# The second score product of a neighbourhood attention, on 64 rows and on all 128

## The chip, the core and the metric

The kernel runs on one core of a Trainium2 chip. The metric is the time of one execution on the device in microseconds (us). The engines named here: TensorE (PE, with its weight loads as PEld), VectorE (DVE), ScalarE (ACT), GpSimd (POOL) and SyncE (SP), whose queue issues all of this kernel's DMAs.

## What is computed

Two layers of a diffusion block work on 512 latent tokens (a grid of 8 rows and 64 columns) and, in the first layer, on 256 context tokens as well. Each layer has a mixer of three kinds side by side (Fourier mixing, retention with four heads, neighbourhood attention with six heads of 64), an output projection and a feed-forward part. The part that matters here:

```python
def neighborhood_attention(q, k, v, k_ctx, v_ctx, rpb):
    ...  # each block of 16 query columns sees a window of 32 key columns in all 8 rows
    s_lat = einsum('brjqhd,brjkhd->bhrjqk', qb, kg) * scale + bias[None]
    s_ctx = einsum('brjqhd,bchd->bhrjqc', qb, k_ctx) * scale
    p = softmax(concatenate([s_lat, s_ctx], axis=-1), axis=-1)
    out = einsum(p_lat, vg) + einsum(p_ctx, v_ctx)
```

In the first layer the context tokens have an attention of their own over the context keys.

## The kernel before

**Split operands.** Products have float32 accuracy from float32r operands: each operand is kept as a high part and a low part, and `mm3` (lines 398 to 400) adds three products, without that of the two low parts. The high part is made by ScalarE (a cast) and the low part by VectorE or GpSimd (a subtraction). For the weights this is `put`: the cast at line 183 (`wh`) and the subtraction at line 188 (`wl`), the latter on GpSimd for nearly all of them.

**The keys and queries of the neighbourhood attention.** A pair of heads shares the 128 rows of a tile, 64 rows each (`HALVES`). `na_evac_q` gives each head a query tile with the high parts in the head's own rows and the low parts in the other 64. `na_evac_k` gives each head a key tile whose high parts stand in both halves (the second by a DMA), and puts the low parts of both heads into one third tile, each in its own rows. So the first product of a score, all 128 rows of the query against the high keys, holds high times high and low times high, and the second needs high times low only: it takes the head's own 64 rows of the query and of the low keys. `mm2` in `score` issues the two (lines 1086 and 1087), and they add up in one PSUM place.

**Blocks.** A head has four blocks of 128 latent queries, and in the first layer a fifth item for the context queries. `score` issues four matmuls for a block: two pairs of 256 columns, or, for the last block of queries (`b == 3`), a pair of 384 and a pair of 128. Then `soft` adds the bias and takes the row's bound on VectorE (line 1074) and the exponent on ScalarE (line 1077), `scale` divides on VectorE (lines 1117 and 1118), `transp` turns the block by four transposes on TensorE (`nt`, line 1129), `parts` splits it (lines 403 and 404, `pt`), and `values` multiplies by the values (`nav`, line 1151). A block is scaled one block later and transposed three blocks later (`NL, SL = 3, 1`).

**The order of the work.** The program's order is written out: `beside` runs two generators side by side, the projections (products `proj`, `v`, `res`) and the attentions, and takes the next piece from the one or the other by the estimated TensorE time and the table `MIX`. So blocks of scores lie between pieces of projections. In each engine the order is fixed by this; the engines wait for each other by semaphores.

**Memory.** Tiles of 768 columns (tag `a`) share 40 places; a tile takes the place of one that is no longer used, and its first writer waits for the last reader of that one. The projected keys of the three pairs are made by `na_proj`, well ahead of their use in `neighbours`.

Of the kernel before, what the change touches and what calls it, by code (L numbers as in the profile page):

```python
# [7 lines left out]
F32 = mybir.dt.float32  # L8
F32R = mybir.dt.float32r
# [18 lines left out]
# feed-forward: pairs of chunks between two returns to the residual stream, by layer  # L28
# [5 lines left out]
# for each layer, where the parts of the attentions lie beside the projections: times after the ends of some;  # L34
# the four heads' retention, the readout, the three pairs' of heads neighbourhoods, the first values
# [5 lines left out]
# steps of the operands' preparation beside the first products  # L41
PREP = (0, 1, 1, 2), (1, 1, 1, 2)
# products of the two-by-two scheme in the order of their use
# half of the latent tokens, in the order of the columns, whose mirror images are the others
# [5 lines left out]
# columns of the vector blob  # L50
V_C, V_BADA, V_GMIX, V_GFFN, V_GFIN, V_RETG, V_DEC, V_SEL, V_RP, V_END = 0, 16, 112, 128, 144, 152, 158, 174, 176, 178
# columns of the constant blob
C_ID, C_BLK, C_END = 0, 128, 256
# columns of the decay strips: latent tiles, edge tile, context-context, context-latent
# [4 lines left out]
class Job:  # L59
    """a pair of chunks of outputs, from pairs of chunks of inputs and for two halves of the tokens, by seven  # L60
    products (Strassen's scheme in Winograd's form):
    P1 = A11 B11, P2 = A12 B21, P3 = S4 B22, P4 = A22 T4, P5 = S1 T1, P6 = S2 T2, P7 = S3 T3,
    S1 = A21 + A22, S2 = S1 - A11, S3 = A11 - A21, S4 = A12 - S2,
    T1 = B12 - B11, T2 = B22 - T1, T3 = B22 - B12, T4 = B21 - T2;
    C11 = P1 + P2, C12 = P1 + P6 + P5 + P3, C22 = P1 + P6 + P7 + P5, C21 = P1 + P6 + P7 + P4"""

# [6 lines left out]
def in_order(jobs, after, window):  # L73
    """the order of the jobs' steps on the tensor engine: the oldest job's first step whose operands are there;
    after[key, step]: pairs of another step and a delay"""
# [26 lines left out]
class WeightStream:  # L102
    """DMA of the weights in the order of their use, running ahead, and their split into two float32r parts."""

    SLOTS = 11
    # the units of a job that the weights of a product are made from
    USES = {1: (0,), 2: (0,), 3: (0,), 4: (1,), 5: (), 6: (0, 1), 7: (0, 1)}

    def __init__(self, kern, raws, parts):
        self.k = kern  # L110
        self.max_raws, self.max_parts = raws, parts
        self.units, self.tasks = [], []
        self.raw, self.parts, self.size, self.pending = {}, {}, {}, []
        self.when = {}
        self.n_dma = self.n_split = self.n_raw = self.n_parts = 0
        self.limit = 10**6
        # products whose weights' second parts are the vector engine's, of the first jobs and the others
        self.lead, self.dve = {}, {}
        # parts that may go to other places, and those that are there
        self.spare, self.away = 0, set()  # L120
# [5 lines left out]
    def add_step(self, job, p, aps):  # L126
        """the weights of one product of a job, from the two units of its outputs"""
# [8 lines left out]
    def issue(self):  # L136
        """start loads while there is room"""
# [28 lines left out]
    def part(self, n):  # L166
        """tiles for the two parts of n columns"""
# [23 lines left out]
    def split(self):  # L191
        """split the next unit, or put it aside for its callback"""
# [18 lines left out]
    def form(self, job, p):  # L211
        """the sums that the weights of product p are made from, and those after it"""
# [9 lines left out]
        if p == 6:  # L222
            # S2 takes the place of A11, S3 that of A21 and S4 that of A12
# [49 lines left out]
    def get(self, key):  # L273
        """the parts of a unit, to be followed by done() after its last use"""
        self.flush()
        self.pump()
        return self.parts.pop(key)
# [7 lines left out]
def beside(first, second, kern):  # L285
    """Run two generators side by side; each yields the tensor-engine time of what it has just emitted,
    which kern.pe adds up. The second also yields spans (from, to, cost): its next work lies between these
    times of the first."""
# [22 lines left out]
def pieces(st):  # L311
    """the latent and the context tokens of a stream: which, columns of all tokens, columns of the stream"""
# [7 lines left out]
class Norm:  # L320
    """a layer norm done step by step: the sums, the rows' factors, then a chunk at a time"""
# [28 lines left out]
class Kern:  # L350
# [10 lines left out]
    # ---- tiles  # L361
    def table(self, key, ap):
        """a table of 1024 columns, loaded ahead of its use"""
# [30 lines left out]
    # ---- products of split operands  # L394
    def mm3(self, out, a, b, start, stop):
        """out += a^T b for a = (hi, lo), b = (hi, lo) without the product of the two low parts"""
# [9 lines left out]
    # ---- set-up  # L406
# [18 lines left out]
    def decay_logs(self):  # L425
        """log_sigmoid of the decay logits: min(x, 0) - 2 atanh(z), z = e / (2 + e), e = exp(-|x|)"""
# [21 lines left out]
    # ---- adaLN modulation  # L448
    def ada_load(self, k):
        """weights of the first layer's first shift and scale for the features 8 p + k"""  # L450
# [9 lines left out]
    def ada_first(self, k):  # L460
        """the two's modulation of the features 8 p + k: four groups of columns of the tensor engine share
        the sums, the rows of one stream are then added and turned to partitions"""
# [39 lines left out]
    def ada_unit(self, layer, part, i):  # L502
        """a unit of the first layer's parts in use before its feed-forward, for the tensor engine;
        of the others, for the vector engine"""
# [7 lines left out]
    def silu_tables(self):  # L512
        """silu of the two conditions on all partitions"""
# [5 lines left out]
    def ada_dve(self, raw, layer, part, i):  # L519
        """modulation of the features 8 p + i: a row's products with the condition, summed"""  # L520
# [69 lines left out]
    # ---- layer norm with modulation  # L590
    def sumsq(self, x, m, acc, st):
        """add the squares of chunk m of the residual stream to the sums of acc, those of the last chunk beside them"""
# [8 lines left out]
    def rstd(self, acc, n, merge=True):  # L601
        """1 / RMS of the n tokens, on all partitions of a bank: roots and reciprocals are taken with
        the tokens on partitions"""
# [18 lines left out]
    def modulate(self, x, rs, st, layer, f, h):  # L622
        """h = x rstd g (1 + sc) + sh, split; a generator over the chunks"""
# [37 lines left out]
    # ---- projections  # L661
    def proj(self, key, h, streams, evac):
        """features on partitions: a chunk of 128 columns of the weight against the streams"""
# [18 lines left out]
    def proj_v(self, keys, h, out, norms=None, late=1, heads=False):  # L682
        """tokens on partitions: 384 columns of the weight for the six token tiles;
        with norms the latent tiles come first, beside the layer norms of the two streams"""
# [27 lines left out]
        if heads:  # L712
            # for each token tile the heads' parts side by side, the second of two heads with its low part first
# [17 lines left out]
    def evac_rope(self, dst, tab):  # L731
        """rotary embedding of the latent tokens; the pairs lie 16 partitions apart"""
# [18 lines left out]
    # ---- retention  # L751
    def strip_piece(self, layer, h, piece, delta, st):
        """decay factors of one piece of the strips, an engine's work at a time: delta holds its distances,
        st takes them"""
# [4 lines left out]
        if piece == "cx":  # L759
            # from the context's state in either direction  # L760
# [13 lines left out]
        # both directions have the diagonal  # L774
# [9 lines left out]
    def pieces(self, work):  # L784
        """strip pieces (layer, head, piece, delta, st), a step behind one another"""
# [16 lines left out]
    def strips_first(self):  # L802
        """the first layer's strips: the first head's stay, the others' go to DRAM"""
# [3 lines left out]
        # the distances  # L807
# [43 lines left out]
    def strips_ahead(self, layer, heads):  # L851
        """strips of a later layer, kept in DRAM"""
# [1393 lines left out]
```

## Time and profile before

| | |
|---|---|
| median of 3 runs | 1755.63 us |
| lowest and highest run | 1754.65 and 1760.47 us |
| span of the profiled execution | 1759.0 us |
| PE busy | 1655.9 us, 94% |
| DVE busy | 1219.6 us, 69% |
| POOL busy | 867.1 us, 49% |
| ACT busy | 744.6 us, 42% |
| mean granted TensorE clock | 0.978 |

The profile is of one execution, so durations from it belong to its span of 1759.0 us and not to the median of the runs. The busy time of an engine is the time in which at least one of its instructions is recorded as running; matmuls overlap in the records, so for PE the distance between the starts of two matmuls says more than their durations. The granted clock is the share of TensorE's full speed that the chip allowed.

### The profile page before, as it was taken

What the parts mean: (1) busy time and instruction counts of PE and PEld (TensorE: products, weight loads), DVE (VectorE), ACT (ScalarE), POOL (GpSimd) and SP (SyncE); (2) the same over time, 40 slices, a digit from 0 to 9 for tenths busy, and PEclk for the clock granted to TensorE, in tenths of its full rate; (3) what the DMA queues carried; (4) which work ended last, traced back from release to release, by engine and by line L of the source; (5) the groups of instructions that cost most, each with busy time, mean ns of one, the idle gap of its engine ahead of it and who ended that gap; (6) DMA issues with size and microseconds to landing.
All of it is one profiled execution on the core that took longest, in us unless ns stands there. A gap on an engine that the chain in (4) does not pass through costs nothing. (4 is left out here: it accounts for less than half of the span.)

```text
span 1759.0 us, 26982 instructions
## 1 busy us (share of the span) xinstructions
PE 1655.9 (94%) x10054; PEld 1481.4 (84%) x10054; DVE 1219.6 (69%) x2040; ACT 744.6 (42%) x1437; POOL 867.1 (49%) x621
## 2 busy tenths in 40 slices
PE   6989999999979998999999999999998799999997
PEld 4867777778978987798999997778788799999997
DVE  6866555664687899586776867764656877767585
ACT  5544434454453223232332554444554444334333
POOL 3343231022467557465665833532035787677673
PEclk9999999999989999999999999999999899999998
DMA  9354243244122343434343444422132232332222
GB/s 344 131 193 133 71 148 94 91 135 167 37 72 85 110 142 108 132 120 132 124 153 114 135 164 138 141 71 87 61 120 73 66 103 87 95 109 84 64 94 72
DMA packets 76387, 202.33 MB, mean 115 GB/s; under 512 B 12704, under 2 KB 19488, under 8 KB 75872
## 3 DMA queue, kind: packets, MB, share of 16 engines
q1 hardware_dynamic: 76256, 200.60, 35.0%
q8 instruction: 80, 1.31, 0.3%
q14 instruction: 51, 0.42, 0.1%
HBM read 184.25 MB, written 11.80 MB: 111 GB/s over the span
## 5 line engine op out<-in xcount | busy, mean ns | idle before, releaser
L188 POOL TENSOR_TENSOR wp<-wr,wp 128x512 fp32r<-128x512 f32 (+1 forms) x336 | 477.5, 1433 | 275.4 <-ACT wp L183 271.8
L399 PE MATMUL f<-hp,wp 128*128 128x384 f32 (+1 forms) x1232 | 387.7, 315 | 13.9 <-POOL wp L188 7.6
L398 PE MATMUL f<-hp,wp 128*128 128x384 f32 (+1 forms) x1232 | 386.9, 314 | 14.5 <-DVE U L1598 5.3
L400 PE MATMUL f<-hp,wp 128*128 128x384 f32 (+1 forms) x1232 | 386.0, 313 | 3.9 <-POOL hp L1523 3.5
L183 ACT CAST wp<-wr 128x512 fp32r<-128x512 f32 (+1 forms) x360 | 213.0, 607 | 355.1 <-PE f L400 117.0
L188 POOL TENSOR_TENSOR wl<-wr,wh 128x1024 fp32r<-128x1024 f32 (+2 forms) x75 | 163.7, 2187 | 379.4 <-ACT wh L183 251.1
L399 PEld LDWEIGHTS f<-hp,wp 128*128 128x128 f32 x1232 | 238.3, 193 | 19.6 <-POOL wp L188 12.9
L398 PEld LDWEIGHTS f<-hp,wp 128*128 128x128 f32 x1232 | 238.6, 194 | 17.8 <-issue 9.7
L400 PEld LDWEIGHTS f<-hp,wp 128*128 128x128 f32 x1232 | 238.4, 194 | 5.2 <-POOL hp L1523 4.3
L398 PE MATMUL f<-g,wp 128*128 128x256 f32 (+1 forms) x576 | 183.6, 319 | 12.8 <-ACT g L1460 12.6
L400 PE MATMUL f<-g,wp 128*128 128x256 f32 (+1 forms) x576 | 183.3, 318 | 4.8 <-POOL g L1461 4.2
L399 PE MATMUL f<-g,wp 128*128 128x256 f32 (+1 forms) x576 | 182.4, 317 | 0.0
L398 PE MATMUL proj<-h,wh 128*128 128x512 f32 (+1 forms) x456 | 167.7, 368 | 0.9 <-DVE v L404 0.9
L399 PE MATMUL proj<-h,wl 128*128 128x512 f32 (+1 forms) x456 | 159.4, 350 | 0.7 <-POOL wl L188 0.7
L400 PE MATMUL proj<-h,wh 128*128 128x512 f32 (+1 forms) x456 | 159.1, 349 | 0.0
L1657 DVE SCALAR_TENSOR_TENSOR x<-f,mod,x 128x256 f32<-128x256 f32 (+1 forms) x160 | 83.8, 546 | 82.8 <-PE f L400 82.7
L398 PEld LDWEIGHTS f<-g,wp 128*128 128x128 f32 x576 | 113.2, 197 | 21.8 <-ACT g L1460 15.2
L400 PEld LDWEIGHTS f<-g,wp 128*128 128x128 f32 x576 | 113.0, 196 | 13.6 <-POOL g L1461 4.8
L399 PEld LDWEIGHTS f<-g,wp 128*128 128x128 f32 x576 | 113.4, 197 | 6.0
L522 DVE CUSTOM_DVE_ANT_0 adj<-wr,tab 128x1024 bf16<-128x1024 f32 x64 | 105.9, 1672 | 10.6 <-DMA wr<-in_w_adat_dram 10.6
L398 PEld LDWEIGHTS proj<-h,wh 128*128 128x128 f32 x456 | 86.6, 190 | 28.6 <-issue 8.3
L399 PEld LDWEIGHTS proj<-h,wl 128*128 128x128 f32 x456 | 86.9, 190 | 11.8 <-POOL wl L188 1.1
(251 smaller groups left out, 3510.1 us busy)
## 6 DMA issues: line engine op xcount, KB each, us to landing
wr<-in_w_dram SPq DMA_DIRECT2D x88, 512.0 KB
wr<-in_w_adat_dram SPq DMA_DIRECT2D x48, 512.0 KB
wr<-in_w_dram SPq DMA_DIRECT2D x80, 256.0 KB
wr<-in_w_ada_dram SPq DMA_DIRECT2D x32, 512.0 KB
ada<-in_w_ada_dram SPq DMA_DIRECT2D x16, 512.0 KB
wr<-in_w_out_dram SPq DMA_DIRECT2D x16, 512.0 KB
tab<-in_rpb_dram SPq DMA_DIRECT2D x12, 512.0 KB
strip<-strips SPq DMA_DIRECT2D x3, 1152.0 KB
```

Of the source, the lines that this page charges most:

```text
L183: nc.scalar.copy(hi, src)
L188: (nc.vector if vector else nc.gpsimd).tensor_sub(lo, src, hi.bitcast(F32))
L398: mm(out, a[0], b[0], start=start, stop=False)
L399: mm(out, a[1], b[0], start=False, stop=False)
L400: mm(out, a[0], b[1], start=False, stop=stop)
L522: self.nc.vector.tensor_tensor_reduce(out=self.tmp(mybir.dt.bfloat16, D, "adj"), in0=raw, in1=self.tabs[("silu", s)], scale=1.0, scalar=0. ...
L1657: k.nc.vector.scalar_tensor_tensor(xs, ps[:, :n], k.mod[:, self.layer, 5, s, m : m + 1], xs, op0=OP.mult, op1=OP.add)
```

## The change

The low parts of the keys get one tile for each head instead of one for the pair. In each, the head's own 64 rows hold the low parts as before, and the other 64 rows are set to zero by GpSimd. The second product of a score then takes all 128 rows of the query tile and of the low keys; the query's low parts meet the zeros. A pair of heads holds four key tiles in place of three. (Comments and docstrings also leave the file; the lines from the middle on have numbers that are one or two higher.)

```diff
     def na_evac_k(self, dst):
...
             for i, (own, other) in enumerate((HALVES, HALVES[::-1])):
                 hi = dst[i][own, c]
+                nc.gpsimd.memset(dst[2 + i][other, c].bitcast(F32), 0.0)
                 nc.scalar.copy(hi, ps[own, :n])
                 nc.sync.dma_start(dst[i][other, c].bitcast(F32), hi.bitcast(F32))
-                nc.vector.tensor_sub(dst[2][own, c], ps[own, :n], hi.bitcast(F32))
+                nc.vector.tensor_sub(dst[2 + i][own, c], ps[own, :n], hi.bitcast(F32))
...
         def score(h, b):
-            r = HALVES[h % 2]
             (q, q3, k), tab = head["qk"], head["tab"]
-            q, q3, kh, kl = q[h % 2], q3[h % 2], k[h % 2], k[2]
+            q, q3, kh, kl = q[h % 2], q3[h % 2], k[h % 2], k[2 + h % 2]
 
             def mm2(out, qb, c0, n):
                 c = slice(c0, c0 + n)
                 nc.tensor.matmul(out, qb, kh[:, c], start=True, stop=False)
-                nc.tensor.matmul(out, qb[r], kl[r, c], start=False, stop=True)
+                nc.tensor.matmul(out, qb, kl[:, c], start=False, stop=True)
...
         def na_proj(c):
...
-            kk = [k.act(F32R, name="nk") for _ in range(3)]
+            kk = [k.act(F32R, name="nk") for _ in range(4)]
```

On TensorE, VectorE, ScalarE and SyncE the instructions stand in the same order as before, with the same tiles' names and shapes of results. GpSimd's queue has 650 rows in place of 626. This is its place in the first layer where the first pair of heads gets its keys (`wl` are low parts of weights, `wr` and `wh` the weights and their high parts; `nq` the last block's queries, `nk` keys, `yr` the retention's readout), before:

```order
L1029 CAST nq_353_1870<-nq_1868 128x128
L1029 CAST nq_354_1871<-nq_1869 128x128
L188 TENSOR_TENSOR wl_1959<-wr_1720,wh_1958 128x768
L1010 TENSOR_TENSOR yr_1904<-yr_1904,osq_1909 128x768
L188 TENSOR_TENSOR wl_2051<-wr_1878,wh_2050 128x768
L1010 TENSOR_TENSOR yr_1905<-yr_1905,osq_1910 128x768
L188 TENSOR_TENSOR wl_2127<-wr_1977,wh_2126 128x768
```

The same place in the changed kernel:

```order
L1029 CAST nq_353_1870<-nq_1868 128x128
L1029 CAST nq_354_1871<-nq_1869 128x128
L188 TENSOR_TENSOR wl_1959<-wr_1720,wh_1958 128x768
L1046 MEMSET nk_1970 64x512
L1046 MEMSET nk_1971 64x512
L1010 TENSOR_TENSOR yr_1904<-yr_1904,osq_1909 128x768
L188 TENSOR_TENSOR wl_2054<-wr_1878,wh_2053 128x768
L1046 MEMSET nk_1970 64x256
L1046 MEMSET nk_1971 64x256
L1010 TENSOR_TENSOR yr_1905<-yr_1905,osq_1910 128x768
L188 TENSOR_TENSOR wl_2132<-wr_1978,wh_2131 128x768
```

Two memsets for the latent tokens (512 columns) and two for the context tokens (256) now stand ahead of a product of the readout and of a weight's low part. GpSimd's queue where the second and the third pair get their keys, before:

```order
L188 TENSOR_TENSOR wl_2516<-wr_2336,wh_2515 128x1024
L188 TENSOR_TENSOR wl_2652<-wr_2519,wh_2651 128x1024
L1029 CAST nq_472_2665<-nq_2663 128x128
L1029 CAST nq_473_2666<-nq_2664 128x128
L188 TENSOR_TENSOR wl_2764<-wr_2538,wh_2763 128x1024
L188 TENSOR_TENSOR wl_2924<-wr_2673,wh_2923 128x528
L188 TENSOR_TENSOR wl_3118<-wr_2783,wh_3117 128x528
```

And in the changed kernel, from the first of the second pair's memsets to the last but one of the third pair's:

```order
L1046 MEMSET nk_2532 64x512
L1046 MEMSET nk_2533 64x512
L188 TENSOR_TENSOR wl_2660<-wr_2524,wh_2659 128x1024
L1046 MEMSET nk_2532 64x256
L1046 MEMSET nk_2533 64x256
L1029 CAST nq_474_2675<-nq_2673 128x128
L1029 CAST nq_475_2676<-nq_2674 128x128
L188 TENSOR_TENSOR wl_2774<-wr_2544,wh_2773 128x1024
L1046 MEMSET nk_2785 64x512
L1046 MEMSET nk_2786 64x512
L188 TENSOR_TENSOR wl_2937<-wr_2683,wh_2936 128x528
L1046 MEMSET nk_2785 64x256
```

Here each low part of a weight has two memsets ahead of it. The second layer has the same pattern, so that 24 memsets are added in all.

## Rows read from the trace of the kernel before

**Rows 1.** The page's first block: busy time, share of the span, instructions.

```profile
span 1759.0 us, 26982 instructions
...
PE 1655.9 (94%) x10054; PEld 1481.4 (84%) x10054; DVE 1219.6 (69%) x2040; ACT 744.6 (42%) x1437; POOL 867.1 (49%) x621
```

**Rows 2.** Two stretches: length; PE, PEld, DVE, ACT, POOL busy; clock, DMA share, GB/s.

```profile
240.00:400.00 160.00, 157.73 (x857) 121.70 (x856) 92.43 (x236) 78.85 (x174) 28.97 (x18) 1.00 0.38 115
1180.00:1300.00 120.00, 117.60 (x603) 93.99 (x602) 67.75 (x160) 59.74 (x124) 26.03 (x17) 0.99 0.23 73
```

**Rows 3.** PE in time: start, duration, line, result and operands, rows*columns, moving operand.

```profile
243.68 0.33 PE L398 MATMUL v<-wh,h 128*128 128x384 f32 x1
...
244.72 0.28 PE L1086 MATMUL ns<-nk,nq 128*128 128x256 f32 x1
244.93 0.38 PE L1087 MATMUL ns<-nk,nq 64*128 64x256 f32 x1
245.24 0.38 PE L1086 MATMUL ns<-nk,nq 128*128 128x256 f32 x1
245.55 0.38 PE L1087 MATMUL ns<-nk,nq 64*128 64x256 f32 x1
245.86 0.44 PE L398 MATMUL v<-wh,h 128*128 128x384 f32 x1
246.14 0.34 PE L399 MATMUL v<-wh,h 128*128 128x384 f32 x1
...
247.01 0.28 PE L1086 MATMUL ns<-nk,nq 128*128 128x256 f32 x1
```

**Rows 4.** PE in time, output projection of the second layer; two more starts lie between.

```profile
1298.64 0.28 PE L400 MATMUL res<-ys,wh 128*128 128x256 f32 x1
...
1298.99 0.28 PE L400 MATMUL res<-ys,wh 128*128 128x256 f32 x1
```

**Rows 5.** PE in time, retention of the second layer; two more starts in each gap.

```profile
1137.11 0.39 PE L398 MATMUL rs<-rq,rk 96*128 96x512 f32 x1
...
1137.80 0.40 PE L398 MATMUL proj<-h,wh 128*128 128x512 f32 x1
...
1138.50 0.40 PE L398 MATMUL rav<-rah,v 128*96 128x512 f32 x1
```

**Rows 6.** PE in time, a block of the last queries; four more starts lie between.

```profile
251.60 0.34 PE L1086 MATMUL ns<-nk,nq 128*128 128x384 f32 x1
...
253.03 0.34 PE L399 MATMUL v<-wh,h 128*128 128x384 f32 x1
```

**Rows 7.** The line of the second product: least, median, greatest duration in ns; forms.

```profile
L1087 PE MATMUL ns<-nk,nq x108: 322/381/442, 244.9 to 1292.6; 64*128 64x256 f32 x84, 64*128 64x384 f32 x12, 64*128 64x128 f32 x12
```

**Rows 8.** Groups of POOL by form: count, busy us, mean ns, idle before and releasers.

```profile
L932 POOL TENSOR_TENSOR ral<-ra,rah 128x512 fp32r<-128x512 f32 x24 | 31.0, 1290 | 65.3 <-ACT rah L931 64.9 <-POOL wl L188 0.3
...
L1029 POOL CAST nq<-nq 128x128 fp32r<-128x128 f32 x12 | 3.5, 292 | 28.7 <-DVE nq L1024 28.7
```

**Rows 9.** In time: a weight's low part, and the first product that takes it.

```profile
287.40 2.40 POOL L188 TENSOR_TENSOR wl<-wr,wh 128x1024 fp32r<-128x1024 f32 x1 [9.08 <-ACT wh L183]
...
317.90 0.39 PE L399 MATMUL proj<-h,wl 128*128 128x512 f32 x1
```

**Rows 10.** PE and DVE in time, second layer; four blocks start 1231.55 to 1236.46.

```profile
1231.55 0.36 PE L1086 MATMUL ns<-nk,nq 128*128 128x256 f32 x1
...
1236.46 0.36 PE L1086 MATMUL ns<-nk,nq 128*128 128x256 f32 x1
1236.63 0.69 DVE L404 TENSOR_TENSOR pt<-nt,pt 128x512 fp32r<-128x512 f32 x1 [0.76 <-ACT pt L403]
...
1239.28 0.69 DVE L404 TENSOR_TENSOR pt<-nt,pt 128x512 fp32r<-128x512 f32 x1 [0.75 <-ACT pt L403]
...
1239.30 0.62 PE L1151 MATMUL nav<-pt,v 128*128 128x512 f32 x1 [1.54 <-ACT pt L403]
```

**Rows 11.** PE in time, first layer: transposes behind a block of scores.

```profile
383.31 0.66 PE L1129 MATMUL nt<-cst,ne 128*128 128x128 f32 x4 [1.40 <-ACT yf L1264]
```

## The prediction

> **What bounds the kernel now.** I read the page's first block first: TensorE (PE) is busy in 1655.9 of 1759.0 us [rows 1]. Such a share says little by itself, because matmuls overlap in the records, so I went to the two stretches in which the changed product runs. The view of stretches shows them: 240 to 400 us (first layer) and 1180 to 1300 us (second layer). There PE is busy 157.7 of 160 and 117.6 of 120 us, VectorE (DVE) 92.4 and 67.8, ScalarE (ACT) 78.9 and 59.7, GpSimd (POOL) 29.0 and 26.0, and the granted clock is 1.00 and 0.99, the higher of its two levels, 2.4 GHz [rows 2]. PE sets the pace there, and every other engine has a third of its time free or more. What PE spends there is therefore on the path unless a reason speaks against it.
>
> Then I read PE's own order of time, by starts and not by durations, because only the distance from one start to the next says what a matmul costs PE. In the first block of scores the reader is to see a break in the rhythm [rows 3]. Products with 128 rows and 384 columns start every 0.173 us (243.68 to 244.72 is six of them). Then come the four matmuls of one score block, 128, 64, 128, 64 rows of 256 columns, at distances of 0.21, 0.31, 0.31 and 0.31 us, and the first product behind them takes 0.28 instead of 0.17. Elsewhere products with 128 rows and 256 columns start 0.35/3 = 0.117 us apart [rows 4]; I use 0.12. The columns are the same and no wait is recorded, so the extra time goes with the passage from 128 rows to 64 and back, in both directions.
>
> Is it the row count, or the weights, or the addition into one PSUM place? Products with 96 rows answer that: three of them and the passage back to 128 rows take 0.69 us (1137.11 to 1137.80), and the next three, with 128 rows, take 0.70 [rows 5]. So fewer than 128 rows cost nothing by themselves, and nor does adding three products into one place, which both kinds do. What stands alone is the 64-row product.
>
> A rule of the Trainium skill fits this: "TensorEngine Tiling (Array Packing)", section "Tiling Modes", says that a change of the tiling mode drains the engine, and a 64-row tile is such a mode. The page gives no price, and none is taken from it.
>
> **The change, part by part.**
>
> *The products.* A block of 256-column products takes 245.86 + 0.28 - 244.72 = 1.42 us from its first start to the second start behind it (246.14) [rows 3]. At the 128-row pace it would be four times 0.12 and once 0.173, which is 0.65. The block gains 0.77 us. The block of the last queries (384 and 128 columns) takes 251.60 to 253.03 = 1.43 us [rows 6]; at the 128-row pace two times 0.173, two times at most 0.12 (a product of 128 columns is not dearer than one of 256), and once 0.173, which is 0.76. It gains 0.67. There are 84 + 12 + 12 products with 64 rows [rows 7], two in a block, so 42 blocks of the first kind and 12 of the second: 42 x 0.77 + 12 x 0.67 = 32.3 + 8.0 = 40.4 us of PE's time. The lower bound of this term is nothing (if the slow pace isn't lifted), the upper is this sum, since the pace behind is that of all other products.
>
> *The zeros.* Each layer has three pairs of heads, each pair two streams and two heads: 24 memsets on POOL, 12 of 64x512 and 12 of 64x256. The trace has no memset of that size. Below it stands the cast of 128x128 with 0.29 us, above it the two-input subtraction of 128x512 with 1.29 [rows 8]; I take 0.6 (a memset reads nothing, so it is nearer to the cast), 14 us in all, 31 at the upper bound. What hides it: POOL is idle 225 of these 280 us [rows 2], and the work queued behind a memset is the weights' low parts (`wl`) and products of the readout. One such low part ends at 289.80 and is first used at 317.90 [rows 9], 28 us later. Without that cover the 14 us (31) would stand on the path. A memset reads no PSUM, so it doesn't wait for PE's product, only for its tile's place to be free. I cost it at nothing.
>
> *The fourth tile of a pair* takes one more place of the pool of 40. The later tiles move by a place each; whoever writes first into a place waits for its last reader. In these stretches PE has almost no idle time [rows 2], so such waits don't reach PE today. I cost it at nothing, up to 1 us.
>
> *The rest.* The 64-row weight loads become 128-row loads, which lie beside the matmul ahead of them as all loads of the 0.12 pace do [rows 4]. VectorE's subtraction writes as many elements as before.
>
> *Where the gain is given back.* The gain arises only where PE isn't waiting for the softmax. In the second layer four blocks follow closely (1231.55 to 1236.46), and then the values wait 1.54 us for ACT [rows 10]. Behind that wait is a ring of VectorE and ACT (bias and minimum, exponent, the cast of the transposed block, and VectorE's subtraction, which waits for that cast): the subtraction stands at 1236.63 and again at 1239.28, so a block takes 2.65 us, while PE sends one every 4.91/3 = 1.64 us. Here a faster PE only waits longer: three blocks at 0.77 and one at 0.67, 3.0 us, are lost. In the first layer one transpose waits 1.40 us for ACT (383.31) just behind a block [rows 11]; that block's 0.8 is lost. Late next is then the second layer's `nav`, by 4.5 us instead of 1.5. For waits that I can't place (the ring elsewhere, a stretch at the lower clock after the longer wait) I take 1.5 us, between nothing and the second rival's loss.
>
> Sum: 40.4 - 3.0 - 0.8 - 1.5 = 35.1 us. The profiled execution has a span of 1759.0 us [rows 1] and would have 1723.9; it lies 3.4 us above the median of the runs, 1755.63, so on the median's scale 1755.6 - 35.1 = 1720.5 us.
>
> **The rivals.**
>
> *The softmax's ring binds widely.* Wherever two blocks would come closer than 2.65 us, PE is held to that. By the starts of the 54 blocks 18 pairs would (the first is 244.72 and 247.01, which would lie 1.52 apart [rows 3]), for 10.1 us together, of which 2.2 lie in the close four that are counted already. For it speaks the ring in [rows 10]; against it that PE transposes a block only three blocks later, which evens such stretches out, and that the first blocks of a layer have no transposes yet, so that their ring is shorter. With all of it the gain is 40.4 - 10.1 - 0.8 - 0.8 (the fourth of the close blocks) = 28.7: 1727 us.
>
> *The slow pace isn't the rows' doing, and padding changes nothing.* Then one pays for four products as before: 1755.6 us, less or more the noise. Against it stand the 96-row products [rows 5] and the 128-row product inside the block that starts 0.31 behind a 64-row one and is as slow as its neighbour [rows 3]. The Trainium skill has a rule on this side: "TensorE: Matmul & The Clock Gate", section "Why this matters for your kernels", says that one matmul with a small K takes as long as one with K = 128, and that only several tiles at once gain. By that rule alone the time would stay at 1755.6. The trace agrees for 96 rows; for 64 rows it differs, 0.31 against 0.12 us, and I follow the trace.
>
> *Slower: the zeros hold POOL's queue, and the weights come late.* A memset stands ahead of the low parts on POOL. If at each of the six pairs half the cover seen in [rows 9] stood, 14 us, the 24 memsets would have to last more than (6 x 14 + 40)/24 = 5.2 us each to eat the cover and the gain; at 6 us they would cost 24 x 6 - 84 = 60 and give 1775 us. The dearest row near it is 1.29 [rows 8], so this needs a memset four times as slow as a subtraction of twice the partitions.
>
> **How the numbers follow.** The forecast, 1720.5 us, gets 0.76; its own range is 1715 (all 40.4 us gained) to 1725. The wide ring gets 0.14, no effect 0.05, the slower case 0.03, and 0.02 is left for a gain that one layer alone gives (about 1738). The range that holds 8 in 10 reaches from 1713 (all gained, and a little less time at the lower clock) to 1731 (the wide ring with some noise). Within 0.3%, 5.3 us, a measurement of this kernel can't be told from no change: the runs before spread by 5.8 us. Faster 0.92, same 0.05, slower 0.03.
>
> **What would show it.** Right: in the profile of the changed kernel the score block's four starts lie 0.12 us apart, and the product behind starts as any other; both stretches together are some 36 us shorter, with PE busy in over 97% of what is left; the 24 memsets last well under 1.3 us and no `wl` is waited for; the `nav` behind the close four blocks waits some 4.5 us. Wrong: starts in the block still 0.2 to 0.3 apart (then the rows aren't the cause), PE's waits in the two stretches grown by 10 us or more (then the ring or the places of the tiles bind), or the stretches shortened as said and the time given back after 400 or 1300 us by a load or a weight whose time doesn't move with PE.

## The result and the profile after

The changed kernel takes 1730.05 us (median of 4 runs, 1728.21 to 1733.25), the kernel before 1756.76 us in the runs beside it (4 runs, 1754.65 to 1760.47). The ratio is 0.984, 95% interval 0.982 to 0.986: 26.7 us less. The forecast was 1720.5 us with a range of 1713 to 1731, so the sign and the wide range hold, but the likeliest value is 9.5 us too low. The time lies outside the forecast's own range (1715 to 1725) and inside the wide one by 1 us, since that made room for the rival with the wide ring (1727), to which the time is closer. Two executions, one of experiment 4 (5481 us) and one of experiment 7 (7663 us), lasted several times as long as the others of the same kernels; the ratios leave them out, and no run explains them.

The page of the changed kernel begins so (span, instructions, then busy time and share of each engine), beside [rows 1]:

```profile
span 1729.9 us, 27017 instructions
...
PE 1620.8 (94%) x10054; PEld 1474.1 (85%) x10054; DVE 1219.4 (70%) x2040; ACT 743.9 (43%) x1437; POOL 876.6 (51%) x645
```

The span is 29.1 us shorter. PE is busy 35.1 us less than before. That this is also the number forecast for the time is a coincidence: the forecast took 40.4 us off PE's work, and work at a lower clock, seen below, lasts longer. 6 us of the 35.1 became idle time of PE.

PE in time, the first block of scores, against [rows 3]:

```profile
243.00 0.28 PE L1087 MATMUL ns<-nk,nq 128*128 128x256 f32 x1
243.12 0.28 PE L1088 MATMUL ns<-nk,nq 128*128 128x256 f32 x1
243.24 0.28 PE L1087 MATMUL ns<-nk,nq 128*128 128x256 f32 x1
243.35 0.28 PE L1088 MATMUL ns<-nk,nq 128*128 128x256 f32 x1
243.47 0.34 PE L398 MATMUL v<-wh,h 128*128 128x384 f32 x1
243.65 0.34 PE L399 MATMUL v<-wh,h 128*128 128x384 f32 x1
```

The break in the rhythm is gone: the four products start 0.12 us apart, and from the first start to the second behind the block it takes 0.65 us in place of 1.42. That is the value the prediction worked with.

The line of the memsets (count; least, median, greatest ns; who waited for it):

```profile
L1046 POOL MEMSET nk<- x24: 304/414/682, 209.2 to 1228.4; 64x512 f32 x12, 64x256 f32 x12
...
  POOL wl L188: 9.5, 2
```

A memset takes 0.30 to 0.68 us, POOL is busy 9.5 us longer in all, and no instruction of PE is in the list of those that waited for one: the two waits in it are GpSimd's own.

PE's waits, first layer (238 to 396 us) and second (1160 to 1270 us), with the time in total, the number and the longest. `fyc` and `fy` are products of the Fourier mixing and `yf` its result, `ne` a block's exponents, `ys` the operand of the output projection:

```profile
PE fyc L398 <- DVE pt L404: 2.1, 1, 2.1
PE res L398 <- ACT ys L1949: 1.5, 1, 1.5
...
PE nt L1130 <- ACT yf L1265: 0.4, 1, 0.4
```

```profile
PE nt L1130 <- DVE ne L1119: 1.9, 1, 1.9
PE nav L1152 <- ACT pt L403: 1.7, 2, 1.4
PE res L399 <- POOL wl L188: 1.1, 1, 1.1
PE fy L400 <- POOL wl L188: 0.8, 1, 0.8
```

Here the missing gain begins to show. The `fyc`, the `nt` for `ne` and the two for `wl` are new; of the transpose's 1.40 us for ScalarE [rows 11] 0.4 is left.

PE executes the same matmuls in the same order in both kernels, so the place of each gain can be found by taking the start of the same matmul in both traces. The length of eight stretches between such starts, which hold all 54 blocks, in us (start and end as in the trace of before; the last two columns are for experiments 5 and 6, in which an exponent is moved):

| stretch before | blocks | length before | after | shorter by | after, exponent moved | before, exponent moved |
|---|---|---|---|---|---|---|
| 244.72 to 320.02 | 15.5 | 75.30 | 64.16 | 11.1 | 62.71 | 74.36 |
| 320.02 to 379.14 | 11.5 | 59.12 | 50.41 | 8.7 | 50.27 | 59.12 |
| 379.14 to 387.69 | 2 | 8.55 | 10.09 | -1.5 | 7.91 | 7.51 |
| 387.69 to 420.06 | 1 | 32.37 | 33.41 | -1.0 | 33.17 | 33.91 |
| 1180.04 to 1231.55 | 9 | 51.50 | 44.79 | 6.7 | 44.71 | 51.50 |
| 1231.55 to 1247.00 | 4 | 15.45 | 15.48 | 0.0 | 13.05 | 12.47 |
| 1247.00 to 1279.94 | 8 | 32.95 | 28.01 | 4.9 | 26.93 | 32.94 |
| 1279.94 to 1299.95 | 3 | 20.01 | 19.99 | 0.0 | 17.54 | 19.76 |

The forecast's 40.4 us are 0.75 us for each block on average. At that price the first two stretches and the fifth, 36 blocks, give 26.9 us, and they gave 26.6. The other five, 18 blocks, should have given 13.5 and gave 2.4. All of the shortfall, about 11 us, lies in these five. The stretches together are 28.9 us shorter; outside them little more than nothing changed.

**The close four blocks** lose their gain to the last hundredth. PE in time after the change, against [rows 10]:

```profile
1206.05 0.37 PE L1087 MATMUL ns<-nk,nq 128*128 128x256 f32 x1
...
1210.51 1.12 PE L1130 MATMUL nt<-cst,ne 128*128 128x128 f32 x4 [1.86 <-DVE ne L1119]
...
1213.88 0.80 PE L1152 MATMUL nav<-pt,v 128*128 128x512 f32 x1 [1.40 <-ACT pt L403]
```

PE arrives earlier and waits 1.86 + 1.40 us in place of 1.54. After the first wait the transposes take 1.12 us in place of 0.60: the clock fell, as the stretches show (length; busy times; granted clock; DMA share, GB/s):

```profile
1204.00:1210.00 6.00, 4.65 (x36) 4.34 (x35) 4.10 (x12) 2.74 (x7) 0.39 (x1) 1.00 0.21 86
1210.00:1218.00 8.00, 6.09 (x22) 5.04 (x23) 5.34 (x15) 4.30 (x11) 0.00 (x0) 0.57 0.01 3
```

From 1210 to 1218 us the granted clock is 0.57, most of it at the lower level, 1.2 GHz; ahead of it PE had waited. VectorE and ScalarE there show why PE waits (`sm` holds a block's row bounds and sums):

```profile
1211.21 0.69 DVE L404 TENSOR_TENSOR pt<-nt,pt 128x512 fp32r<-128x512 f32 x1 [0.75 <-ACT pt L403]
1211.81 0.68 DVE L1076 CUSTOM_DVE_ANT_1 ne<-ns,tab 128x512 f32<-128x512 f32 x1
...
1212.61 0.49 DVE L1119 TENSOR_SCALAR ne<-ne,sm 128x512 f32<-128x512 f32 x1
1213.86 0.69 DVE L404 TENSOR_TENSOR pt<-nt,pt 128x512 fp32r<-128x512 f32 x1 [0.76 <-ACT pt L403]
```

```profile
1212.54 0.72 ACT L1079 ACTIVATE ne<-ne,sm 128x512 f32<-128x512 f32 x1 [1.36 <-DVE sm L1076]
...
1213.26 0.57 ACT L403 CAST pt<-nt 128x512 fp32r<-128x512 f32 x1
```

VectorE's subtraction stands at 1211.21 and 1213.86, 2.65 us apart, the very ring of before. In its 2.65 us VectorE is idle 0.75, waiting for ScalarE's cast; that cast stands behind the exponent, and the exponent waits for VectorE's own row bound of the next block (1211.81). The two engines wait for each other by turns.

**The last three blocks** are held by the same thing, which the prediction didn't see. ScalarE in time:

```profile
1257.30 0.73 ACT L1079 ACTIVATE ne<-ne,sm 128x512 f32<-128x512 f32 x1 [2.29 <-DVE sm L1076]
...
1260.55 0.72 ACT L1079 ACTIVATE ne<-ne,sm 128x512 f32<-128x512 f32 x1 [1.47 <-DVE sm L1076]
...
1261.27 0.62 ACT L183 CAST wh<-wr 128x528 fp32r<-128x528 f32 x1
...
1263.73 0.72 ACT L1079 ACTIVATE ne<-ne,sm 128x512 f32<-128x512 f32 x1 [1.36 <-DVE sm L1076]
```

In the kernel before these three exponents start 3.24 and 3.19 us apart (1287.70, 1290.94, 1294.13), here 3.25 and 3.18. This chain didn't get faster, and the weight's cast at 1261.27 stands in it; GpSimd's `wl` follows at 1262.02, and `fy` waits for that. So the wait named for `wl` comes out of ScalarE's queue and not from the zeros; experiments 5 and 9 test that for both waits.

**The end of the first layer**, the third and the fourth stretch, lost by another mechanism. VectorE and GpSimd in time, ahead of `fyc`:

```profile
355.22 0.19 DVE L573 TENSOR_TENSOR modg<-modg 128x32 f32<-128x32 f32 x1 [1.61 <-DMA modg<-adad]
...
355.66 2.28 DVE L582 TENSOR_TENSOR mod<-modg,vec 128x8 f32<-128x8 f32 x1
...
359.27 0.68 DVE L404 TENSOR_TENSOR pt<-nt,pt 128x512 fp32r<-128x512 f32 x1
```

```profile
355.54 2.39 POOL L188 TENSOR_TENSOR wl<-wr,wh 128x1024 fp32r<-128x1024 f32 x1 [2.44 <-issue]
```

```profile
360.00 0.39 PE L398 MATMUL fyc<-wh,fph 128*128 128x256 f32 x1 [2.14 <-DVE pt L404]
```

VectorE first waits 1.61 us for a DMA. Before, it came there 19 us later in the span (374.34) and didn't wait. Then its sum of 128x8 takes 2.28 us (0.17 in the kernel before, at 374.77) and ends together with GpSimd's subtraction, 357.94 and 357.93. So `pt` comes late, PE waits 2.14 us, and the granted clock from 357.57 to 367.67 is 0.83.

The fourth stretch has a fall of the clock of its own. The first row is the changed kernel, behind the 1.5 us that `res` waits for `ys`; the second is the kernel before, around the same wait at 410.65 (columns as above):

```profile
388.00:396.00 8.00, 6.12 (x28) 4.00 (x26) 3.25 (x7) 2.46 (x6) 0.00 (x0) 0.79 0.10 27
```

```profile
405.00:420.00 15.00, 12.90 (x72) 10.11 (x73) 6.18 (x12) 6.54 (x12) 3.85 (x2) 1.00 0.43 159
```

The wait is the same in both traces, and the clock fell in one. It fell there in experiment 6 too, which has no padded rows (0.89 from 405 to 420 us; 33.91 us for the stretch in place of 32.37), so this part of the loss can't be called the padding's own, and what decides it stays open. By the two clocks, (1 - 0.83) x 10.1 and (1 - 0.79) x 8 us, each of the two falls costs PE an estimated 1.7 us.

The Trainium skill has a rule for the sum that was held, in "SBUF — State Buffer", section "Who interferes with whom": a VectorE instruction with two operands in SBUF contends with a GpSimd instruction that reads SBUF, not with one that only writes it. The trace agrees on the first half, since both instructions take two operands from SBUF and the sum was held until the subtraction ended. The other half no row here singles out.

### The profile page after: what moved, and what is told of

Its sections match the earlier page's. It is cut to its first block, busy times and chain, and to the rows that moved or that the text cites. A ratio compares the mean times of both kernels' runs of the same rounds, so it can differ in the third digit from the quotient of the medians.

```text
span 1729.9 us, 27017 instructions
## 1 busy us (share of the span) xinstructions
PE 1620.8 (94%) x10054; PEld 1474.1 (85%) x10054; DVE 1219.4 (70%) x2040; ACT 743.9 (43%) x1437; POOL 876.6 (51%) x645
## 3 DMA queue, kind: packets, MB, share of 16 engines
q8 instruction: 80, 1.31, 0.3%
## 5 line engine op out<-in xcount | busy, mean ns | idle before, releaser
L398 PEld LDWEIGHTS f<-g,wp 128*128 128x128 f32 x576 | 113.4, 197 | 22.3 <-ACT g L1461 15.5
```

Source lines behind the costliest of these rows:

```text
L398: mm(out, a[0], b[0], start=start, stop=False)
```

## The experiments

**1. Half the passages.** The kernel before, with the order of the second pair turned:

```diff
-                nc.tensor.matmul(out, qb, kh[:, c], start=True, stop=False)
-                nc.tensor.matmul(out, qb[r], kl[r, c], start=False, stop=True)
+                two = [(qb, kh[:, c]), (qb[r], kl[r, c])]
+                for j, (x, y) in enumerate(two[::-1] if flip else two):
+                    nc.tensor.matmul(out, x, y, start=j == 0, stop=j == 1)
```

> The kernel before (64-row second products), but in the second pair of a block the product of the low keys comes first, so that the two 64-row products meet in the middle: 128, 64, 64, 128 rows in place of 128, 64, 128, 64. The same four products, two passages between 128 and 64 rows in place of four. Theory P (the passage costs, 0.77/4 = 0.19 us each): the start of the second 64-row product lies 0.12 us behind the first, a block loses 0.39 us in place of 0.77, the 54 blocks gain 42 x 0.39 + 12 x 0.34 = 20.4 us, less the give-back, which took 11 of 40 us of the full change; so 14 to 20 us, 1736 to 1743 us. Theory B (each 64-row product is slow by itself, whatever stands beside it): no change, 1751 to 1760 us, and the two 64-row products start about 0.3 us apart. Theory S (the second product into one PSUM place is what is slow): no change either, but the last 128-row product is as slow as the 64-row one.

Measured: 1742.44 us (6 runs), ratio 0.992 (0.989 to 0.994), 15.1 us less than the 1757.57 beside it. PE in time, the first block:

```profile
243.64 0.28 PE L1088 MATMUL ns<-nk,nq 128*128 128x256 f32 x1
243.85 0.38 PE L1088 MATMUL ns<-nk,nq 64*128 64x256 f32 x1
244.07 0.28 PE L1088 MATMUL ns<-nk,nq 64*128 64x256 f32 x1
244.28 0.38 PE L1088 MATMUL ns<-nk,nq 128*128 128x256 f32 x1
244.50 0.34 PE L398 MATMUL v<-wh,h 128*128 128x384 f32 x1
244.68 0.33 PE L399 MATMUL v<-wh,h 128*128 128x384 f32 x1
```

The block takes 244.68 - 243.64 = 1.04 us, half way between 1.42 and 0.65, with the same four products. So the cost is that of the passage, 0.19 us each, and not of the 64-row product: theory P. One sign of that theory didn't come: the second 64-row product starts 0.22 us behind the first and not 0.12. The starts in the block are 0.21, 0.22, 0.21 and 0.22 us apart. They come out if a passage delays its own start by 0.09 us and the next start by 0.10, and with that estimate so do those of before (0.21, three times 0.31, then 0.28 in place of 0.17). The price of a passage is thus spread over two starts.

**2 and 3. One layer alone.** `kk` has four tiles in one layer and three in the other, and `score`, `na_evac_k` follow the number:

```diff
-            kk = [k.act(F32R, name="nk") for _ in range(4)]
+            kk = [k.act(F32R, name="nk") for _ in range(4 if layer == 0 else 3)]
```

> Padded low keys in the first layer alone; the second layer has the 64-row products and the shared tile of before. Theory A (the layers' gains add up): the first layer's own gain as the traces give it, 17.3 us, and nothing else: 1737 to 1742 us. Rival (what the first layer gains is partly spent because the second layer also starts earlier against its loads, or the reverse): more than 4 us away from 1739.

> Padded low keys in the second layer alone; the first layer is as before. Theory A (the layers add up): 11.6 us, 1742 to 1747 us, and the waits of the close four blocks (about 3.6 us) and the two waits for a weight's low part on GpSimd (about 2 us) stand there as in the full change. Rival (those two waits come from the shift of the first layer): they are gone, and this layer gains 13 to 15 us, 1740 to 1742.

Measured: first layer alone 1740.55 us (ratio 0.990, 0.988 to 0.991), 17.0 us less; second layer alone 1747.7 us (0.994, 0.993 to 0.996), 9.9 less, 0.7 above the expected range. Together 26.9 against 26.7. PE's waits of the second layer, padded alone:

```profile
PE nt L1132 <- DVE ne L1121: 1.9, 1, 1.9
PE nav L1154 <- ACT pt L403: 1.7, 2, 1.4
PE res L399 <- POOL wl L188: 1.1, 1, 1.1
```

They are those of the full change to the tenth, with the first layer as before. Each layer's loss is made in that layer; the layers add up.

**4 and 9. Four times the zeros.**

```diff
-                nc.gpsimd.memset(dst[2 + i][other, c].bitcast(F32), 0.0)
+                for _ in range(4):
+                    nc.gpsimd.memset(dst[2 + i][other, c].bitcast(F32), 0.0)
```

> The changed kernel with each of the 24 memsets issued four times into the same place: 72 more, about 0.4 us each, 30 us more on GpSimd. Theory H (the zeros are hidden): 1727 to 1734 us, as the changed kernel. Rival Z (the zeros made the weights' low parts late, and the two waits for them in the second layer, 2 us, are their price): those waits grow by three times as much, 1736 us or more.

> Each memset four times, once more, for a trace: the earlier profiled execution of this kernel lasted 5481 us, three times its other runs, with every matmul slow. Theory H (the zeros are hidden): 1727 to 1735 us, and TensorE's two waits for wl stay at 0.8 and 1.1 us. Rival Z: they grow to 3 us or more each.

Measured: 1732.5 and, again, 1730.45 us (ratios 0.985, 0.983 to 0.987, and 0.984, 0.983 to 0.986). The trace of the second:

```profile
L1047 POOL MEMSET nk<- x96: 304/494/772, 209.3 to 1230.9; 64x512 f32 x48, 64x256 f32 x48
...
  DVE nq L1024: 0.7, 1
```

GpSimd is busy 30.7 us longer than in the changed kernel, PE's two waits for `wl` are 0.8 and 1.1 us as before, and the one wait for a memset is 0.7 us of VectorE. The zeros are hidden, with room for four times as many.

**5 and 6. The exponent behind the cast.** In `neighbours`, ScalarE's exponent of a block is put behind `parts` of the same round; nothing else moves. Experiment 6 is the same edit in the kernel before.

```diff
-            nc.scalar.activation(dst, dst, AF.Exp, bias=s[:, 0:1], scale=-1.0, accum_out=s[:, 1:2])
+            later.append((dst, s))
...
                 if b > 0 or h == 0:
                     parts(b)
+            exps()
```

> The changed kernel, with the exponent of a block (ScalarE) issued behind the cast of the block that is turned in the same round, in place of ahead of it; the work is the same, TensorE, VectorE and GpSimd keep their order. In the changed kernel VectorE's subtraction of the turned block waits 0.75 us in every block of the close four, because ScalarE's cast stands behind the exponent, which waits for VectorE itself; and a weight's cast (wh), on which GpSimd's low part and then TensorE wait, stands behind such an exponent at 1261.27. Theory R (this ring of VectorE and ScalarE eats the second layer's gain): the waits of nt (1.9), nav (1.4) and of the two products for wl (1.9) go, and half of the 6.8 us at the lower clock: 4 to 7 us less than the changed kernel, 1723 to 1726 us. Rival L (the exponent is then late itself, behind casts that wait for TensorE): new waits of the same size, 1729 us or more.

> The same move of the exponent in the kernel before, with its 64-row products. There the ring shows in one wait of 1.5 us and 3.4 us at the lower clock behind it. Theory R: a gain of 1.5 to 3.5 us, 1753 to 1756 us, smaller than the move's gain in the changed kernel; so with the ring out of the way the padded rows bring more than the 27 us that they bring with it, 30 to 34. Rival L: no gain in either, and the difference stays at 27.

Measured: the changed kernel with this edit takes 1720.62 us (ratio 0.978, 0.977 to 0.979), 9.4 us less than without it; no version here is faster. The kernel before was slower beside it than beside the changed kernel, 1759.03 against 1756.76 us; by the differences from it, 38.4 and 26.7, the edit brings 11.7 us. The kernel before with it takes 1756.68 (0.998, 0.997 to 0.999 against 1759.03), 2.3 us less. So with the exponent moved in both the padded rows bring 1756.68 - 1720.62 = 36.1 us, more than expected. VectorE in time, the close four blocks of experiment 5:

```profile
1205.90 0.68 DVE L404 TENSOR_TENSOR pt<-nt,pt 128x512 fp32r<-128x512 f32 x1
...
1207.70 0.68 DVE L404 TENSOR_TENSOR pt<-nt,pt 128x512 fp32r<-128x512 f32 x1
```

A block now takes 1.80 us on VectorE in place of 2.65, and the wait for the cast is gone. In the column of experiment 5 the three stretches that the ring had held are shorter by 2.43, 1.08 and 2.45 us, 6.0 in all. Not all of that is the padding's: the same edit shortens the close four blocks of the kernel before by 2.98 us, from 15.45 to 12.47. With the exponent moved in both, the padding gains 6.0 us in the eight blocks and 2.2 in the last three, its full price, but in the close four still nothing (12.47 and 13.05). PE's waits of the second layer:

```profile
PE nt L1135 <- DVE ne L1124: 1.9, 1, 1.9
PE nav L1157 <- DVE pt L404: 0.7, 1, 0.7
```

Theory R holds for both waits for `wl`, which are gone, and for `nav`, whose wait for ScalarE is gone and of which 0.7 us for VectorE are left. It doesn't hold for `nt`, whose 1.9 us stay: there VectorE itself is behind, with two subtractions at 1203.49 ahead of the row bound for that block. Another 2.2 us came back between 379.14 and 387.69: the sum of 128x8 takes 0.17 us again (352.82), as GpSimd's subtraction falls elsewhere. That part is a change of timing and not the ring. The 1.45 us by which the first stretch is shorter were not followed; in the kernel before the edit gives 0.94 there.

**7 and 8. The modulation later.** The six small operations of `ada_sum` are put 5000 ns of the program's estimated time later, in the changed kernel (7) and in that of experiment 5 (8):

```diff
-                self.w.pending.append((lambda _: self.ada_sum(part, got), None, 0.0))
+                self.w.pending.append((lambda _: self.ada_sum(part, got), None, self.pe + 5000.0))
```

> The changed kernel, with VectorE's six small operations on the modulation (modg, mod, gs), which wait 1.6 us for a DMA at 355.22 and then stand 2.3 us beside GpSimd's subtraction, put one block and a half later in VectorE's order; nothing else moves. Theory M (they make the subtraction pt late for which TensorE waits 2.1 us at 360, and the lower clock from 360.6 follows from that wait): the wait and the stretch at the lower clock go, 2.5 to 4 us less than the changed kernel, 1726 to 1728 us. Rival K (VectorE is late there anyway): the wait stays over 1 us, 1729 to 1732 us.

> Both moves in the changed kernel, the exponent behind the cast and the modulation later. If theories R and M hold and their gains add up: 1718 to 1723 us. If only one holds: 1723 to 1728.

Measured: 1732.04 us (0.985, 0.984 to 0.986) and 1721.25 us (0.978, 0.977 to 0.980), no gain in either. In the trace of 7 the wait of `fyc` and the lower clock behind it are gone, so VectorE's delay caused the wait, and in this one trace the clock went with it. But others took their place:

```profile
PE nt L1130 <- ACT yf L1265: 2.0, 1, 2.0
...
PE nt L1130 <- DVE yn L1158: 0.8, 1, 0.8
```

The first grew from 0.4, the second is new, as is one of 0.5 us of `nav`, and the clock of the fourth stretch fell again (0.86 from 388 to 400 us). The mechanism was right, the expected time wrong: the end of the first layer has a second limit directly behind the first.

**10. 96 rows.** In the changed kernel the second product of the even heads takes `r = slice(0, 96)`.

> The changed kernel, but the second product of heads 0, 2 and 4 takes 96 of the 128 rows (the 64 with low keys and 32 of the zeros); heads 1, 3 and 5 all 128. Theory W (only products of 64 rows make a passage, 96 rows run as 128, which the retention's products of before suggest): 1727 to 1734 us as the changed kernel, a 256-column block of an even head takes 0.65 us. Rival (any change of the row count costs 0.19 us): half of the blocks lose 0.77 us again, 21 us less some waits, 1744 to 1751 us.

Measured: 1726.95 us (0.982, 0.980 to 0.984), 3.1 us less than the changed kernel, with intervals that overlap. PE in time, a block with 96 rows:

```profile
243.09 0.28 PE L1088 MATMUL ns<-nk,nq 128*128 128x256 f32 x1
243.21 0.28 PE L1089 MATMUL ns<-nk,nq 96*128 96x256 f32 x1
243.33 0.29 PE L1088 MATMUL ns<-nk,nq 128*128 128x256 f32 x1
```

The starts lie 0.12 us apart. Between 128 and 96 rows there is no passage to pay, between 128 and 64 there is: theory W. In this trace neither fall of the clock at the end of the first layer came (1.00 from 357 to 366 and from 388 to 396 us, in place of 0.81 and 0.79), and `fyc` waited 1.31 us in place of 2.14. So the loss there is not the same in every version with padded rows.

**11. One block more of lag.** Experiment 5 with `NL, SL = 4, 1`.

> The changed kernel with the exponent behind the cast, and a block transposed four blocks after its scores in place of three (NL = 4). Theory R2 (what is left of the ring is one block's lag: nt waits 1.9 us for ne in the second layer and 1.7 us for yf in the first): both waits shrink to under 0.5 us, 2 to 4 us less than with the exponent's move alone, 1716.5 to 1719 us. Rival (the values come a block later and the projections that wait for them too; a fifth block in flight needs places): 1720 us or more.

Measured: 1729.88 us (0.984, 0.982 to 0.986), 9.3 us more than experiment 5, as the rival has it. In the second layer PE no longer waits 1.9 us for `ne`, but the values wait instead (1.9 us for VectorE's `pt`, 1.2 for ScalarE's), and in the first layer new waits for VectorE stand beside them. Where the rest goes wasn't followed.

## Why the prediction was right, and by what it missed

**The price of the passage held.** A block gains 0.77 us as worked out, 36 of the 54 blocks gave their full price, and experiments 1 and 10 show the cause that the rows of before had suggested: the passage between 128 and 64 rows, 0.19 us, whichever way it goes. The second rival (padding changes nothing) is refuted. The rule of the Trainium skill that stood beside it, "TensorE: Matmul & The Clock Gate", section "Why this matters for your kernels", has a single matmul with K = 32 (the rows of the product) take as long as one with K = 128. At 96 rows the traces show the like (0.12 us a start). A 64-row product between 128-row ones costs 0.38 us more with its two passages, which that rule leaves out; what a 64-row product takes in a longer row of such products no run here shows.

**The zeros and the fourth tile held.** The memsets take 0.41 us at the median (0.6 taken) and are hidden, also four times over. No wait that I could put down to a tile's place shows among PE's waits, but no run tested the fourth tile by itself. The slower rival had nothing in it.

**The give-back was mis-sized: 5.3 us forecast, about 11.5 found.** The term for the close four blocks, 3.0 us, is right to a tenth; its reason holds only in part, since with the exponent moved (experiments 5 and 6) they still gain nothing from the padding, and there VectorE itself is behind. The term of the first layer's transpose, 0.8 us, fell short: the two stretches from 379.14 to 420.06 lose 1.5 + 1.5 own gain and 1.0 + 0.8, about 4.8 us. The wait for ScalarE that I named shrank there by 1.0 us. A new one of 2.1 us for VectorE came ahead of it, out of a DMA and a subtraction beside which VectorE stood, and the clock fell twice, behind that wait and behind the one of `res`. These are 1.1 us of waits and an estimated 3.4 us at the lower clock, 4.5 of the 4.8. The term "waits that I can't place", 1.5 us, stands for 3.2 us of the second layer and 0.5 elsewhere: the last three blocks lose all their 2.2 us, the eight ahead of them 1.0, to the ring. I had looked at the ring only where PE already waited for it, and not where it ran without slack. The exponents 3.2 us apart at 1290 us were in the trace of before.

**The wide-ring rival** came near the size of the give-back, 11.7 us, by luck as much as by its reason. It expected 10.1 us from pairs of blocks in both layers; the stretches that the ring held lost 6.2 us, all in the second layer. Only 3.2 of these, the eight blocks and the last three, come back when the ring is loosened; the other 3.0, in the close four, don't. The rest of the give-back is, but for 0.5 us, that of the end of the first layer.

**From 1720.5 to 1730.05**: 6.0 us are the larger give-back (35.1 against 29.1 by the spans), 2.4 the difference between the two profiled executions and the medians (29.1 against 26.7), 1.1 the higher median of before in the later runs.

Of the signs that I named, the starts and the short memsets came as said. "No `wl` is waited for" did not (1.1 and 0.8 us, by ScalarE's queue and not by the zeros), nor did "both stretches 36 us shorter" (28.9) and "PE busy over 97%" (96 and 94). The `nav` wait was shared between `nt` and `nav`, 3.26 us; the rest went into the lower clock. Open stay the 1.5 us that `res` waits for `ys` in both kernels, and why a lag of four blocks costs so much.

## What to carry to other kernels

Read matmuls by the distance of their starts, and where a row count changes between neighbours, price the change and not the product: here 0.19 us for each passage between 128 and 64 rows, nothing between 128 and 96. When a busy engine is made faster, look for the places where a ring of other engines already runs without slack, even if nothing waits there yet; the last three blocks gave back their whole gain, 2.2 us, at one where PE had not waited. Here the ring was one of order: putting an instruction that waits behind one that could run brought 9.4 us or more with the change and 2.3 without it, so an edit that was worth little may be worth trying again after the bottleneck has moved.

## What was unexpected

A VectorE sum of 128x8 elements, 0.17 us by itself, took 2.28 us beside GpSimd's subtraction of 128x1024 and ended with it; in experiment 5 a scaling of 128x512 took 2.48 us in place of 0.49, seen below, with such a subtraction running from 355.52 to 357.90. In the two traces it was not the same instruction that was hit.

```profile
355.70 2.48 DVE L1124 TENSOR_SCALAR ne<-ne,sm 128x512 f32<-128x512 f32 x1
```
